# An adaLN trunk with two gated linear attentions: the gate's row as rounded parts, squares added by VectorE, and a free list that ranks tiles behind a store later

## The chip, the cores and the metric

One core of one Trainium2 chip runs the whole layer for one sequence. The metric is the device time of one execution in microseconds (us). Before the change three executions took 1219.83, 1215.38 and 1220.5 us, median 1219.83.

## The reference, cut to what matters

The width is D = 1024, the sequence T = 1024, and there is one layer. All values are fp32.

```python
mod = c_act @ ada_w[l] + ada_b[l]
shift, scale, gate = jnp.split(mod, 3, axis=-1)
h = rms_norm(x, norm_w[l]) * (1.0 + scale[:, None, :]) + shift[:, None, :]
proj = h @ w_in[l]
hq, hf, hi, hz, gq, gk, gv, gz, ga, mg = jnp.split(proj, IN_OFFSETS, axis=-1)
y_h = hgrn2_branch(hq, hf, hi, hz, lb_all[l], hgrn_norm_w[l])   # 8 heads, normed over all 1024
y_g = gla_branch(gq, gk, gv, gz, ga, gla_alpha_w[l], gla_alpha_b[l], gla_norm_w[l])   # 4 heads, normed per head
u_h = y_h @ w_branch[l, 0]
u_g = y_g @ w_branch[l, 1]
mg = jax.nn.sigmoid(mg.reshape(B, T, N_BRANCH, D_MODEL))
merged = mg[:, :, 0] * u_h + mg[:, :, 1] * u_g
x = x + gate[:, None, :] * (merged @ w_out[l])
return rms_norm(x, final_norm_w)
```

## The kernel before

**Products.** A product of fp32 matrices is done as three matmuls of rounded parts (type fp32r): hi x hi, hi x lo and lo x hi. `split` (L186 to L198) makes the parts: ScalarE (ACT) casts to hi (L196), VectorE (DVE) subtracts hi to get lo (L197). Weights get the same at L1285 and L1286 (`prep_duo`), factors of the gate stages at L1260 to L1264 (`build`).

**Order of the work.** A stream of jobs feeds TensorE (PE) with the input projection, one column block after another (`Feat`, its matmuls at L541; `Vblk`, L600 to L602; `Vblk2`, L643 to L645). Between the groups of a job's matmuls `Stream.weave` advances two tracks of generators, whose yielded numbers are a wait in such groups. One track holds the attention heads (`attention`, L657 on, with its score matmuls at L715 and on, copies to `scT` at L790 to L796, then `gla_attention` or `hgrn_attention`). The other, in the background, holds `prepare`, which makes differences of activations (`factors`) and sums of weights (`weight_sums`) and stores them to DRAM, and `gate_side`, which computes the row `gate`. After the stream come four gate stages (`last_stages`, matmuls at L1343): the two halves of `mg` for the two gates, and the two branch projections. Each is a product of 2 x 2 blocks done with seven block products instead of eight, on the stored sums and differences. The first, b = 0, makes the second branch's gate: `put_gate1` takes the sigmoid (L1414) and stores the result (L1415) to DRAM, to be loaded again two stages later. The next, b = 1, makes the other gate (`put_gate0`). Last comes the output projection (`out_stage`, L1520). From the text of the kernel a scheduler derives the order of the instructions of each engine; dependences become semaphores.

**Queues.** Loads are issued by SyncE (SP), in order, so a load that waits holds those behind it. Stores are issued by GpSimd (POOL): `put_act` (L916) for the heads' outputs, `factors` (L1167), `weight_sums` (L1201), `put_gate1` (L1415), `keep_wy` (L1469).

**Slots.** All larger tiles, 46 slots of 4 KB per partition, come from `Slots` (L35 to L53). Freed slots go to the end of a queue, and `get` takes its head: the slot that was freed first. Freeing happens in the text of the kernel, not in time. Whoever writes the next tile in a slot waits for the last readers of the former one, and a store that sends the former tile to DRAM is such a reader. `Halves` (L56 to L80) hands out halves of a slot.

**The gate's row.** In `gate_side` DVE sums eight rows of blocks of `ada_w`, weighted with the conditioning, into `gacc` (L1054, 128 partitions x 1024). Then, for each half of the row, PE sums the partitions and adds the bias with two matmuls in fp32: `ones` x `gacc` (L1062) and one row of `ones` x `gbias` (L1063). ACT copies the result (L1064).

**Squares.** A GLA head has two tiles of squares, added by POOL (L987); the eight HGRN heads add theirs to one tile, by POOL too (L1107, seven adds). Both are followed, at once or at the last head, by `inverse_root`, which splits the sum and sums its partitions on PE. A tile of squares is freed behind its add.

Of the kernel before, what the change touches and what calls it, by code (L numbers as in the profile page):

```python
# [2 lines left out]

# [31 lines left out]
class Slots:  # L35


    def __init__(self, pool, n):
        self.pool = pool
        self.free_list = deque(range(n))  # L40
        self.owner = {}
        self.serial = 0

    def get(self, shape, dtype=F32):
        i = self.free_list.popleft()
        self.serial += 1
        t = self.pool.tile([P] + list(shape), dtype, tag=f"s{i}", name=f"b{self.serial}")
        self.owner[id(t)] = (i, t)
        return t

    def free(self, *tiles):
        for t in tiles:
            self.free_list.append(self.owner.pop(id(t))[0])  # L53


class Halves:  # L56
# [5 lines left out]
    def get(self):  # L62
        if not self.open:
            t = self.slots.get([2, 512])
            left = [0, t]
            self.open.extend((t[:, i, :], left) for i in range(2))
        v, left = self.open.popleft()
        left[0] += 1
        self.owner[id(v)] = (v, left)
        return v  # L70

    def free(self, *views):
        for v in views:
            v, left = self.owner.pop(id(v))
            left[0] -= 1
            if left[0]:
                self.open.append((v, left))
            else:
                self.open = deque(z for z in self.open if z[1] is not left)
                self.slots.free(left[1])  # L80


@with_exitstack
def hybrid_trunk_kernel(
# [6 lines left out]
    nc = tc.nc  # L91
# [822 lines left out]
    def put_act(acts, d, y):  # L914
        for half in range(2):
            nc.gpsimd.dma_start(acts[half][d // 2][:, d % 2 * 512:d % 2 * 512 + 512], y[:, half * 512:half * 512 + 512])  # L916
        S.free(y)

    def alpha_side():
        lower_bound()  # L920
# [49 lines left out]
    def gla_attention(h):  # L970
        qk = g_state
        v = qk.pop(("v", h))
        g = {}
        sq = {}

        def post(vh, half, po):
            if half == 0:
                g[vh] = qk.pop(("z", h, vh))
                sq[vh] = S.get([T])
            sl = slice(half * 512, half * 512 + 512)  # L980
            nc.scalar.activation(sq[vh][:, sl], po, AF.Square)
            nc.vector.scalar_tensor_tensor(g[vh][:, sl], po, vec[:, R_GN + vh:R_GN + vh + 1],
                                           g[vh][:, sl], ALU.mult, ALU.mult)

        yield from attention(qk.pop(("q", h)), qk.pop(("k", h)), alphas[h], lambda: v, 0, 256, post)
        S.free(*v)
        nc.gpsimd.tensor_add(sq[0], sq[0], sq[1])  # L987
        yield 1.5
        rst = sq[1]
        yield from inverse_root(rst, sq[0], 256)  # L990
        for half in range(4):
            sl = slice(half * 256, half * 256 + 256)
            for vh in range(2):
                nc.vector.tensor_mul(g[vh][:, sl], g[vh][:, sl], rst[:, sl])
            yield 1.5
        for vh in range(2):
            put_act(yg_d, 2 * h + vh, g[vh])
        S.free(*sq.values())
# [45 lines left out]
    def gate_side():  # L1044

        gacc, gbias = S.get([D]), S.get([D])
        nc.sync.dma_start(gbias[0:1, :], ada_b[0:1, 2 * D:3 * D])
        for k in range(KT):
            b = S.get([D])
            nc.sync.dma_start(b, ada_w[0, k * P:(k + 1) * P, 2 * D:3 * D])  # L1050
            if k == 0:
                nc.vector.tensor_scalar_mul(gacc, b, cs[:, 0:1])
            else:
                nc.vector.scalar_tensor_tensor(gacc, b, cs[:, k:k + 1], gacc, ALU.mult, ALU.add)  # L1054
            S.free(b)
            yield 1
        yield 3
        gate_b[0] = S.get([D])
        for half in range(2):
            sl = slice(half * 512, half * 512 + 512)  # L1060
            pg = mtile()
            nc.tensor.matmul(pg, ones, gacc[:, sl], start=True, stop=False)  # L1062
            nc.tensor.matmul(pg, ones[0:1, :], gbias[0:1, sl], start=False, stop=True)  # L1063
            nc.scalar.copy(gate_b[0][:, sl], pg)  # L1064
        S.free(gacc, gbias)


    h_state = {}
# [17 lines left out]
    def hgrn_attention(h):  # L1086
        st = h_state
        y = [None]
        sq = [None]

        def post(vh, half, po):
            if half == 0:
                y[0], sq[0] = st.pop(("z", h)), S.get([T])
            sl = slice(half * 512, half * 512 + 512)
            nc.scalar.activation(sq[0][:, sl], po, AF.Square)
            nc.vector.scalar_tensor_tensor(y[0][:, sl], po, vec[:, R_HN + h:R_HN + h + 1],
                                           y[0][:, sl], ALU.mult, ALU.mult)

        yield from attention(st.pop(("q", h)), st.pop(("k", h)), st.pop(("f", h)), lambda: st[("v", h // 4)],
                             h % 4 * P, P, post, 4 if h % 4 == 1 else 3)  # L1100
        if h % 4 == 3:
            S.free(*st.pop(("v", h // 4)))
        put_act(yh_d, h, y[0])
        if ssq[0] is None:
            ssq[0] = sq[0]
        else:
            nc.gpsimd.tensor_add(ssq[0], ssq[0], sq[0])  # L1107
            S.free(sq[0])
        if h == 7:
            yield 2  # L1110
            rst = S.get([T])
            yield from inverse_root(rst, ssq[0], D)
            S.free(ssq[0])
            rst_h[0] = rst
# [40 lines left out]
    def factors(acts, f):  # L1155
        sub = nc.vector.tensor_sub
        for kk in range(2):
# [7 lines left out]
            for p, dst, a, b in ((5, "11", "12", "11"), (7, "12", "12", "22"), (6, "22", "22", "11"), (4, "21", "21", "22")):  # L1165
                sub(y[dst], y[a], y[b])
                nc.gpsimd.dma_start(f[p][kk], y[dst])  # L1167
                if p == 7:
                    S.free(y["12"])
                elif p == 6:  # L1170
                    S.free(y["11"])
                yield 1.5
            S.free(y["22"], y["21"])

    def branch(n, d):
        return w_branch[0, n, :, d * P:(d + 2) * P]
# [6 lines left out]
    def weight_sums(b, i):  # L1183
# [16 lines left out]
        for p, q in SUMS.items():  # L1200
            nc.gpsimd.dma_start(w_sums[b][i // 2][q][:, i % 2 * 512:i % 2 * 512 + 512],  # L1201
                                parts[p].rearrange("p k f -> p (k f)"))
        S.free(x1, x2, s1, s2)
        yield 3

    def prepare():
# [83 lines left out]
    class Banks:  # L1290
# [11 lines left out]
        def free(self, v):  # L1302
            self.free_list.append(v)
# [108 lines left out]
    def put_gate1(d, half, ap, summed):  # L1412
        g = ap if summed else Q.get()
        nc.scalar.activation(g, ap, AF.Sigmoid)  # L1414
        nc.gpsimd.dma_start(gate1_d[d][:, half * 512:half * 512 + 512], g)  # L1415
        Q.free(g)

    def put_gate0(d, half, ap, summed):
        nc.scalar.activation(merged(d, half), ap, AF.Sigmoid)
# [65 lines left out]
        keep_wy(p, kk, *dst)  # L1485

    def drop_wy():
        S.free(*wy.values())
        wy.clear()

    def load_w4(p):
# [191 lines left out]
    stream.hooks[1, 4] = begin_2  # L1683
    stream.go()
    S.free(*h_hi, *h_lo)
    lent = [dtile() for _ in range(2)]
    R.lend([pd[:, i * 512:i * 512 + 512] for pd in lent[::-1] for i in range(2)])
    last_stages()
# [30 lines left out]
```

## Time and profile before

| | before |
|---|---|
| profiled execution, whole | 1216.46 us |
| its span, first to last instruction | 1214.8 us |
| granted TensorE clock | 0.998 |
| PE busy | 1184.1 us, 97% |
| DVE, ACT, POOL busy | 790.9, 546.9, 123.8 us |
| input projection and attention until about | 806 us |
| gate stages and branch projections, then output | 806 to 1214.8 us |

A row of the timeline reads: start, duration (both in us from the start of the span), engine, line, operation, written tile <- read tiles, sizes and type, count, and in brackets how long its engine had been idle and what ended that. Buffer numbers are left out, so most tiles are called `b`; `pd`, `pm` and `sc_ps` are PSUM tiles. PEld is PE's loading of weights, SPq the issuing of loads by SP. A wait for several semaphores is put down to the one that came last.

### The profile page before, as it was taken

The page shows a single profiled execution, that of the slowest core. Times are in us where ns is not written, and L with a number is a line of the kernel's source. Part 1 is how long each engine was busy: PE and PEld are TensorE (multiplying, and loading weights), DVE is VectorE, ACT ScalarE, POOL GpSimd, SP SyncE. Part 2 cuts the span into 40 slices and gives each one's busy share as a digit, 9 for nine tenths or more (in the row PEclk, how much of TensorE's full clock was granted, in tenths as well). Part 3 has the DMA queues.
Part 4 walks back from the last instruction along what each step waited for, and adds up shares of the span by engine and source line. Part 5 has one row for each costly group of instructions (what it writes and reads, how often), then busy time and mean ns, then how long its engine had stood idle before and what let it go on. Part 6 is the DMA issues. An engine that isn't in the chain of part 4 may idle for free.

```text
span 1214.8 us, 20860 instructions
## 1 busy us (share of the span) xinstructions
PE 1184.1 (97%) x8579; PEld 982.6 (81%) x8579; DVE 790.9 (65%) x1245; ACT 546.9 (45%) x797; POOL 123.8 (10%) x215
## 2 busy tenths in 40 slices
PE   5999999999999999999999999999999999999997
PEld 3777889889798888888887888877778888878886
DVE  4637444774848456877884365794653775988994
ACT  5646732434434244344332324455743544444554
POOL 4100000202111121121110101011220000000000
PEclk9999999999999999999999999999999999999999
DMA  9814000844444267255341112054697746435523
GB/s 320 277 70 139 18 19 19 293 141 161 156 152 149 66 207 249 94 179 169 108 174 47 59 53 70 36 174 158 227 343 277 260 160 208 135 104 173 174 104 122
DMA packets 130961, 183.51 MB, mean 151 GB/s; under 512 B 7467, under 2 KB 97633, under 8 KB 130866
## 3 DMA queue, kind: packets, MB, share of 16 engines
q1 hardware_dynamic: 117250, 136.87, 35.7%
q0 software_dynamic: 13568, 45.31, 9.6%
q8 instruction: 67, 1.10, 0.4%
q14 instruction: 28, 0.23, 0.1%
q10 hardware_dynamic: 48, 0.01, 0.0%
HBM read 132.87 MB, written 49.28 MB: 150 GB/s over the span
## 4 chain that ended last, share of the span: by engine, by line
PE 61%; issue 23%; DVE 3%; ACT 3%; POOL 2%; DMA 1%; POOLq 0%; ACTq 0%; DVEq 0%
PE pd L541 19%; PE pd L1343 9%; PE sc_ps L1343 5%; PE pm L1343 5%; PE pd L1520 3%; PE pd L643 2%; PE pd L644 2%; PE pd L645 2%; PE sc_ps L1520 2%; PE pm L848 1%; PE pd L352 1%; PE pm L829 1%; PE pm L850 1%; PE pm L1520 1%; PE sc_ps L352 1%
## 5 line engine op out<-in xcount | busy, mean ns | idle before, releaser
L541 PE MATMUL pd<-b,b 128*128 128x512 f32 x1632 | 387.4, 394 | 0.0
L541 PEld LDWEIGHTS pd<-b,b 128*128 128x128 f32 x1632 | 302.4, 188 | 64.8 <-issue 1.4
L1343 PE MATMUL pd<-b,b 128*128 128x512 f32 x720 | 173.7, 392 | 4.3 <-ACT b L1414 2.1
L1343 PEld LDWEIGHTS pd<-b,b 128*128 128x128 f32 x720 | 133.7, 188 | 35.7 <-ACT b L1414 3.2
L197 DVE TENSOR_TENSOR b<-b,b 128x1024 fp32r<-128x1024 f32 (+2 forms) x89 | 98.9, 1122 | 83.1 <-ACT b L196 65.4
L196 ACT CAST b<-b 128x1024 fp32r<-128x1024 f32 (+2 forms) x89 | 82.9, 948 | 92.1 <-DVE b L1199 14.6
L1286 DVE TENSOR_TENSOR b<-b,b 128x1024 fp32r<-128x1024 f32 x56 | 68.3, 1224 | 66.9 <-ACT b L1285 52.3
L1285 ACT CAST b<-b 128x1024 fp32r<-128x1024 f32 x56 | 58.3, 1050 | 73.9 <-PE pd L1343 20.6
L1343 PE MATMUL sc_ps<-b,b 128*128 128x512 f32 x324 | 79.4, 391 | 1.0 <-ACT scT L793 1.0
L600 PE MATMUL pd<-b,b 128*128 128x256 f32 x256 | 74.2, 290 | 0.0
L1264 DVE TENSOR_TENSOR b<-b,b 128x1024 fp32r<-128x1024 f32 x48 | 59.2, 1251 | 20.8 <-ACT b L1263 15.1
L602 PE MATMUL pd<-b,b 128*128 128x256 f32 x256 | 72.5, 283 | 0.0
L601 PE MATMUL pd<-b,b 128*128 128x256 f32 x256 | 72.4, 283 | 0.0
L1343 PEld LDWEIGHTS sc_ps<-b,b 128*128 128x128 f32 x324 | 60.3, 188 | 14.6 <-ACT scT L793 1.4
L1343 PE MATMUL pm<-b,b 128*128 128x512 f32 x300 | 72.1, 389 | 0.0
L1263 ACT CAST b<-b 128x1024 fp32r<-128x1024 f32 x48 | 49.9, 1050 | 41.2 <-PE pd L1343 16.0
L1343 PEld LDWEIGHTS pm<-b,b 128*128 128x128 f32 x300 | 56.3, 188 | 11.7
L352 PE MATMUL pd<-b,b 128*128 128x512 f32 x192 | 53.3, 410 | 2.0 <-ACT b L196 0.9
L1201 POOL DMA_DIRECT2D ws<-b x64 | 34.6, 541 | 192.0 <-DVE b L1195 86.5
L735 ACT COPY xb<-b 128x512 f32<-128x512 f32 x48 | 29.4, 620 | 49.4 <-PE sc_ps L715 26.7
L643 PE MATMUL pd<-b,b 128*128 128x512 f32 x128 | 51.3, 401 | 0.0
L644 PE MATMUL pd<-b,b 128*128 128x512 f32 x128 | 50.0, 390 | 0.0
(285 smaller groups left out, 1964.3 us busy)
## 6 DMA issues: line engine op xcount, KB each, us to landing
b<-in_w_in_dram SPq DMA_DIRECT2D x66, 512.0 KB, 4.2
ws<-b POOLq DMA_DIRECT2D x64, 256.0 KB, 3.3
b<-ws SPq DMA_DIRECT2D x32, 512.0 KB, 4.9
b<-in_x_dram SPq DMA_DIRECT2D x16, 512.0 KB, 5.7
b<-in_ada_w_dram SPq DMA_DIRECT2D x32, 256.0 KB, 6.9
b<-in_w_branch_dram SPq DMA_DIRECT2D x16, 512.0 KB, 4.4
b<-h SPq DMA_DIRECT2D x14, 512.0 KB, 4.3
wo<-b POOLq DMA_DIRECT2D x14, 512.0 KB, 5.7
```

The source lines that it names most:

```text
L196: nc.scalar.copy(hi, src)
L197: nc.vector.tensor_sub(lo, src, hi.bitcast(F32))
L352: nc.tensor.matmul(accs[f], wg(a, d, f), b[d][:, half * 512:half * 512 + 512], start=(d == 0 and n == 0), stop=(d == KT - 1 and n == 2))
L541: nc.tensor.matmul(ps[0:w, th * 512:(th + 1) * 512], a[:, k, 0:w], b[:, th * 512:(th + 1) * 512], start=(k == 0 and n == 0), stop=(k == KT ...
L600: nc.tensor.matmul(o, lh, hi[:, k % 4, :], start=(k == 0), stop=False)
L601: nc.tensor.matmul(o, lh, lo[:, k % 4, :], start=False, stop=False)
L602: nc.tensor.matmul(o, ll, hi[:, k % 4, :], start=False, stop=(k == KT - 1))
L643: nc.tensor.matmul(o, lh, hi[:, k % 2, :], start=(k == 0), stop=False)
L644: nc.tensor.matmul(o, lh, lo[:, k % 2, :], start=False, stop=False)
L1286: nc.vector.tensor_sub(lo, t, hi.bitcast(F32))
L1343: nc.tensor.matmul(o, a[:, sl], c, start=(p in (1, 5) and kt == 0 and n == 0), stop=(kt == 3 and n == 2), skip_group_check=True)
L1520: nc.tensor.matmul(o, a, b, start=(p in (1, 5) and kt == 0 and n == 0), stop=(kt == 3 and n == 2), skip_group_check=True)
```

## The change

It has three parts.

1. *Gate's row.* DVE adds the bias to the first partition's row of `gacc`, `split` makes hi and lo of the sum (ACT and DVE), and four fp32r matmuls, `ones_r` x hi and `ones_r` x lo for each half, take the place of four fp32 ones. Two more slots are taken for it, and the generator yields 4 instead of 3 ahead of the matmuls.
2. *Squares.* The eleven adds go from POOL to DVE.
3. *Free list.* It becomes a heap, ranked by the count of tiles handed out at the time of freeing. Tiles that a store still reads are marked `sent` and get `S.behind` added to their rank. `S.behind` is 0 until the stream has ended, where the order is that of the queue before, and 8 from the gate stages on.

```diff
--- before.py
+++ after.py
@@ -1,3 +1,4 @@
+import heapq
 from collections import deque
 from contextlib import ExitStack
 
@@ -37,20 +38,22 @@
 
     def __init__(self, pool, n):
         self.pool = pool
-        self.free_list = deque(range(n))
+        self.free_list = [(-1, i - n, i) for i in range(n)]
+        self.freed = self.behind = 0
         self.owner = {}
         self.serial = 0
 
     def get(self, shape, dtype=F32):
-        i = self.free_list.popleft()
+        i = heapq.heappop(self.free_list)[-1]
         self.serial += 1
         t = self.pool.tile([P] + list(shape), dtype, tag=f"s{i}", name=f"b{self.serial}")
         self.owner[id(t)] = (i, t)
         return t
 
-    def free(self, *tiles):
+    def free(self, *tiles, sent=False):
         for t in tiles:
-            self.free_list.append(self.owner.pop(id(t))[0])
+            self.freed += 1
+            heapq.heappush(self.free_list, (self.serial + (self.behind if sent else 0), self.freed, self.owner.pop(id(t))[0]))
 
 
 class Halves:
@@ -62,22 +65,23 @@
     def get(self):
         if not self.open:
             t = self.slots.get([2, 512])
-            left = [0, t]
+            left = [0, t, False]
             self.open.extend((t[:, i, :], left) for i in range(2))
         v, left = self.open.popleft()
         left[0] += 1
         self.owner[id(v)] = (v, left)
         return v
 
-    def free(self, *views):
+    def free(self, *views, sent=False):
         for v in views:
             v, left = self.owner.pop(id(v))
             left[0] -= 1
+            left[2] |= sent
             if left[0]:
                 self.open.append((v, left))
             else:
                 self.open = deque(z for z in self.open if z[1] is not left)
-                self.slots.free(left[1])
+                self.slots.free(left[1], sent=left[2])
 
 
 @with_exitstack
@@ -914,7 +918,7 @@
     def put_act(acts, d, y):
         for half in range(2):
             nc.gpsimd.dma_start(acts[half][d // 2][:, d % 2 * 512:d % 2 * 512 + 512], y[:, half * 512:half * 512 + 512])
-        S.free(y)
+        S.free(y, sent=True)
 
     def alpha_side():
         lower_bound()
@@ -984,7 +988,7 @@
 
         yield from attention(qk.pop(("q", h)), qk.pop(("k", h)), alphas[h], lambda: v, 0, 256, post)
         S.free(*v)
-        nc.gpsimd.tensor_add(sq[0], sq[0], sq[1])
+        nc.vector.tensor_add(sq[0], sq[0], sq[1])
         yield 1.5
         rst = sq[1]
         yield from inverse_root(rst, sq[0], 256)
@@ -1054,15 +1058,18 @@
                 nc.vector.scalar_tensor_tensor(gacc, b, cs[:, k:k + 1], gacc, ALU.mult, ALU.add)
             S.free(b)
             yield 1
-        yield 3
+        nc.vector.tensor_add(gacc[0:1, :], gacc[0:1, :], gbias[0:1, :])
+        hi, lo = split(gacc)
+        S.free(gacc, gbias)
+        yield 4
         gate_b[0] = S.get([D])
         for half in range(2):
             sl = slice(half * 512, half * 512 + 512)
             pg = mtile()
-            nc.tensor.matmul(pg, ones, gacc[:, sl], start=True, stop=False)
-            nc.tensor.matmul(pg, ones[0:1, :], gbias[0:1, sl], start=False, stop=True)
+            nc.tensor.matmul(pg, ones_r, hi[:, sl], start=True, stop=False)
+            nc.tensor.matmul(pg, ones_r, lo[:, sl], start=False, stop=True)
             nc.scalar.copy(gate_b[0][:, sl], pg)
-        S.free(gacc, gbias)
+        S.free(hi, lo)
 
 
     h_state = {}
@@ -1104,7 +1111,7 @@
         if ssq[0] is None:
             ssq[0] = sq[0]
         else:
-            nc.gpsimd.tensor_add(ssq[0], ssq[0], sq[0])
+            nc.vector.tensor_add(ssq[0], ssq[0], sq[0])
             S.free(sq[0])
         if h == 7:
             yield 2
@@ -1166,11 +1173,11 @@
                 sub(y[dst], y[a], y[b])
                 nc.gpsimd.dma_start(f[p][kk], y[dst])
                 if p == 7:
-                    S.free(y["12"])
+                    S.free(y["12"], sent=True)
                 elif p == 6:
-                    S.free(y["11"])
+                    S.free(y["11"], sent=True)
                 yield 1.5
-            S.free(y["22"], y["21"])
+            S.free(y["22"], y["21"], sent=True)
 
     def branch(n, d):
         return w_branch[0, n, :, d * P:(d + 2) * P]
@@ -1200,7 +1207,8 @@
         for p, q in SUMS.items():
             nc.gpsimd.dma_start(w_sums[b][i // 2][q][:, i % 2 * 512:i % 2 * 512 + 512],
                                 parts[p].rearrange("p k f -> p (k f)"))
-        S.free(x1, x2, s1, s2)
+        S.free(x1, x2)
+        S.free(s1, s2, sent=True)
         yield 3
 
     def prepare():
@@ -1413,7 +1421,7 @@
         g = ap if summed else Q.get()
         nc.scalar.activation(g, ap, AF.Sigmoid)
         nc.gpsimd.dma_start(gate1_d[d][:, half * 512:half * 512 + 512], g)
-        Q.free(g)
+        Q.free(g, sent=True)
 
     def put_gate0(d, half, ap, summed):
         nc.scalar.activation(merged(d, half), ap, AF.Sigmoid)
@@ -1485,7 +1493,7 @@
         keep_wy(p, kk, *dst)
 
     def drop_wy():
-        S.free(*wy.values())
+        S.free(*wy.values(), sent=True)
         wy.clear()
 
     def load_w4(p):
@@ -1683,6 +1691,7 @@
     stream.hooks[1, 4] = begin_2
     stream.go()
     S.free(*h_hi, *h_lo)
+    S.behind = 8
     lent = [dtile() for _ in range(2)]
     R.lend([pd[:, i * 512:i * 512 + 512] for pd in lent[::-1] for i in range(2)])
     last_stages()
```

Three places of the resulting order. On PE, at the matmuls of the gate's row (`pm` the sum, `pd` the tile of the job in the stream), before:

```order
L644 MATMUL pd_5955<-b_5712,b_150 128x512
L645 MATMUL pd_5955<-b_5711,b_158 128x512
L1062 MATMUL pm_6017<-b_5918,ones 128x512
L1063 MATMUL pm_6017<-b_5919,ones 128x512
L1062 MATMUL pm_6021<-b_5918,ones 128x512
L1063 MATMUL pm_6021<-b_5919,ones 128x512
L643 MATMUL pd_6026<-b_5699,b_143 128x512
L644 MATMUL pd_6026<-b_5700,b_143 128x512
```

and now, where lines of the file are a few higher:

```order
L648 MATMUL pd_6022<-b_5700,b_143 128x512
L649 MATMUL pd_6022<-b_5699,b_151 128x512
L647 MATMUL pd_6022<-b_5699,b_144 128x512
L648 MATMUL pd_6022<-b_5700,b_144 128x512
L649 MATMUL pd_6022<-b_5699,b_152 128x512
L1069 MATMUL pm_6030<-b_5999,ones_r 128x512
L1070 MATMUL pm_6030<-b_6000,ones_r 128x512
L1069 MATMUL pm_6034<-b_5999,ones_r 128x512
L1070 MATMUL pm_6034<-b_6000,ones_r 128x512
L647 MATMUL pd_6022<-b_5703,b_145 128x512
```

The four have moved behind six matmuls of the next `pd` tile, and read the two parts.

On ACT, at the start of the gate stages (L1260 and L1268 the rounding of a factor's part 3, L1285 and L1293 the cast of weights, L1414 and L1422 the sigmoid, L1317 and L1325 a copy of a finished bank, L735 and L739 copies for a head), before:

```order
L1317 ACTIVATE b_7505<-pd_7440 128x512
L1317 ACTIVATE b_7601<-pd_7441 128x512
L735 COPY xb<-b_7164 128x512
L735 COPY xb<-b_7330 128x512
L735 COPY xb<-b_7164 128x512
L735 COPY xb<-b_7330 128x512
L1317 ACTIVATE b_7601<-pd_7441 128x512
L1414 ACTIVATE b_7638<-pd_7440 128x512
L1260 ACTIVATE b_7823<-b_7755 128x1024
L1414 ACTIVATE b_7731<-pd_7440 128x512
L1285 CAST b_7913<-b_7807 128x1024
L790 COPY scT<-sc_ps 32x4x32 x4
```

and now:

```order
L1268 ACTIVATE b_7828<-b_7760 128x1024
L1325 ACTIVATE b_7606<-pd_7446 128x512
L739 COPY xb<-b_7169 128x512
L739 COPY xb<-b_7335 128x512
L739 COPY xb<-b_7169 128x512
L739 COPY xb<-b_7335 128x512
L1325 ACTIVATE b_7606<-pd_7446 128x512
L1422 ACTIVATE b_7643<-pd_7445 128x512
L1293 CAST b_7871<-b_7743 128x1024
L1422 ACTIVATE b_7736<-pd_7445 128x512
L1293 CAST b_7918<-b_7812 128x1024
L794 COPY scT<-sc_ps 32x4x32 x4
```

The second rounding, of `b_7823` and now `b_7828`, stands ahead of the copies to `xb` instead of behind the first sigmoid, and where it stood is a cast of weights.

On SP, late in the first gate stage (`fx` stored factors, `ws` stored sums, `in_w_in_dram` weights), before:

```order
L1230 DMA b_8082<-fx_736 128x1024
L1278 DMA b_8061<-in_w_in_dram 128x4x128 x2
L1230 DMA b_8081<-fx_735 128x1024
L1278 DMA b_8110<-in_w_in_dram 128x4x128 x2
L1278 DMA b_8159<-in_w_in_dram 128x4x128 x2
L1278 DMA b_8200<-in_w_in_dram 128x4x128 x2
L1466 DMA b_8328<-in_w_out_dram 128x2x512
L1274 DMA b_8347<-ws_749 128x1024
L1278 DMA b_8237<-in_w_in_dram 128x4x128 x2
```

and now:

```order
L1238 DMA b_8086<-fx_735 128x1024
L1238 DMA b_8087<-fx_736 128x1024
L1286 DMA b_8066<-in_w_in_dram 128x4x128 x2
L1286 DMA b_8115<-in_w_in_dram 128x4x128 x2
L1286 DMA b_8205<-in_w_in_dram 128x4x128
L1286 DMA b_8164<-in_w_in_dram 128x4x128 x2
L1286 DMA b_8205<-in_w_in_dram 128x4x128
L1286 DMA b_8242<-in_w_in_dram 128x4x128 x2
L1282 DMA b_8312<-ws_745 128x1024
```

The two loads of `b_8159`, now `b_8164`, stood third and fourth of six; now one of the two loads of the next tile, `b_8205`, stands ahead of them. Its slot is one that a gate store reads.

## Prediction

> **What bounds the kernel now.** I read the page's totals first, then its slices, then the list of PE's waits, then the timeline at each place where the change or a wait stands.
>
> ```profile
> span 1214.8 us, 20860 instructions
> ...
> PE 1184.1 (97%) x8579; PEld 982.6 (81%) x8579; DVE 790.9 (65%) x1245; ACT 546.9 (45%) x797; POOL 123.8 (10%) x215
> ...
> PE   5999999999999999999999999999999999999997
> ...
> PEclk9999999999999999999999999999999999999999
> ```
>
> TensorE (PE) is busy for 97% of the span, full in every slice but the first and the last, and its clock is full throughout. So a change gains where it takes a matmul away, or where it ends one of PE's few waits. What it does on VectorE (DVE, 65%), ScalarE (ACT, 45%) and GpSimd (POOL, 10%) counts only if PE stands still for it. The list of PE's waits (engine, tile and line <- releaser: total, times, longest) says where it does:
>
> ```profile
> PE pd L1343 <- ACT b L1414: 2.1, 2, 1.8
> PE pd L1343 <- DVE b L953: 1.5, 1, 1.5
> ...
> PE sc_ps L1343 <- ACT scT L793: 1.0, 1, 1.0
> ...
> PE pd L1343 <- DVE b L1435: 0.4, 1, 0.4
> ...
> PE sc_ps L715 <- DVE blk L698: 0.2, 1, 0.2
> PE pd L1343 <- ACT b L1315: 0.2, 1, 0.2
> ```
>
> These six are all waits that can belong to the gate stages or to attention heads near an edit; together 5.4 us. The other rows of the list lie at lines that the change doesn't touch. More than 5.4 us can therefore come only from matmuls that cost less.
>
> **The gate's row** is the one place where PE itself gets less work. The timeline of before (start, duration, engine, line, tiles):
>
> ```profile
> 640.47 0.39 PE L644 MATMUL pd<-b,b 128*128 128x512 f32 x1
> ...
> 640.69 0.39 PE L645 MATMUL pd<-b,b 128*128 128x512 f32 x1
> ...
> 640.92 1.02 PE L1062 MATMUL pm<-b,ones 128*128 128x512 f32 x2
> 641.12 1.01 ACT L648 COPY b<-pd 128x1024 f32<-128x1024 f32 x1 [9.86 <-PE pd L645]
> ...
> 641.87 1.12 PE L1063 MATMUL pm<-b,ones 1*128 1x512 f32 x2
> ...
> 644.08 1.04 ACT L196 CAST b<-b 128x1024 fp32r<-128x1024 f32 x1 [0.47 <-PE pm L1062]
> ...
> 645.02 0.50 PE L643 MATMUL pd<-b,b 128*128 128x512 f32 x1
> 645.19 1.23 DVE L197 TENSOR_TENSOR b<-b,b 128x1024 fp32r<-128x1024 f32 x1 [6.22 <-ACT b L196]
> ```
>
> From 640.92 to 645.02 PE does four fp32 products, each in two passes: 4.10 us. The fp32r matmuls ahead of them follow each other at 640.47, 640.69 and 640.92, so every 0.225 us. Four of that kind take 0.90 us: **-3.2 us**. They now need hi and lo of the summed row. The chain: the last of the five accumulations ends at 632.41 + 6.56 = 638.97,
>
> ```profile
> 632.41 6.56 DVE L1054 SCALAR_TENSOR_TENSOR b<-b,cs,b 128x1024 f32<-128x1024 f32 x5
> ```
>
> then the add of the bias (I take the 1.23 us of a 128x1024 DVE operation, though it is one row), the cast (1.04) and the subtraction (1.23): 642.5. The order of instructions puts the four matmuls six later, that is at 640.92 + 6 x 0.225 = 642.3, and the first of them needs hi alone. So the chain is just in time. ACT is idle for 9.86 us before 641.12, so the cast finds it free. Were the copy of 641.12 in front, lo would come at about 644.4 and PE would lose 1.9 of the 3.2 again. Bounds -3.2 to -1.3; I take **-3.1**.
>
> **The eleven adds that go from POOL to DVE.** Such an add is 2.4 us on POOL, and beside each a DVE instruction is long. Two of them, with the group that shows the usual length of one of these DVE lines:
>
> ```profile
> 284.78 2.40 POOL L987 TENSOR_TENSOR b<-b,b 128x1024 f32<-128x1024 f32 x1 [1.16 <-ACT b L981]
> 285.40 2.33 DVE L1198 TENSOR_TENSOR b<-b,b 128x512 f32<-128x512 f32 x1
> 798.04 2.75 POOL L1107 TENSOR_TENSOR b<-b,b 128x1024 f32<-128x1024 f32 x1
> 799.10 2.21 DVE L679 TENSOR_TENSOR xb<-xb,b 128x256 f32<-128x256 f32 x1
> L1198 DVE TENSOR_TENSOR b<-b,b 128x512 f32<-128x512 f32 x16 | 12.6, 788 | 0.1
> ```
>
> Of 16 at L1198 the one beside POOL takes 2.33, so the other 15 take (12.6 - 2.33) / 15 = 0.68: the neighbour loses 1.6 us. On DVE the add itself should take 1.2 us, as the other 128x1024 operations do. Net per add between -0.4 and, if the neighbour's length had another cause, +1.2; I take -0.3, by the rows. The Trainium skill, SBUF — State Buffer, "Who interferes with whom", says that a VectorE instruction with two SBUF inputs and a GpSimd instruction that reads SBUF exclude each other for a whole instruction. By it the neighbour's loss is POOL's doing and goes with the add (the trace agrees: 285.40 + 2.33 ends 0.55 us after POOL's 287.18, about the instruction's own 0.68); without it DVE would carry 11 x 1.2 = 13 us more.
>
> Elsewhere than at 812 us PE has DVE's result in hand, so a few tenths either way cost nothing there; the 0.2 at L698 stays as it is. At 812 DVE has been behind since 799:
>
> ```profile
> 810.62 1.23 DVE L953 TENSOR_TENSOR b<-b,pd 128x1024 f32<-128x1024 f32 x1
> 811.90 1.43 PE L1343 MATMUL pd<-b,b 128*128 128x512 f32 x5 [1.49 <-DVE b L953]
> ```
>
> L953 frees a PSUM bank for which PE waits 1.49. The stretch at 799.10 (2.21, of a kind that is 256 columns wide and so at most the 0.68 of L1198) goes, an add of 1.2 comes: L953 ends 0.3 earlier. But ACT now has a cast ahead of the copy that frees the neighbouring bank. **-0.2**, bounds -1.5 (the wait goes) to +1.2.
>
> **The free list.** Slots that a store still reads are handed out later, so waits for a store move from ACT to other places. Three of ACT's waits stand just before waits of PE. First:
>
> ```profile
> 828.34 1.06 ACT L1260 ACTIVATE b<-b 128x1024 fp32r<-128x1024 f32 x1 [3.59 <-DMA gate<-b]
> 829.43 1.23 DVE L1261 SCALAR_TENSOR_TENSOR b<-b,b 128x1024 fp32r<-128x1024 f32 x1 [0.58 <-ACT b L1260]
> 832.15 1.06 ACT L790 COPY scT<-sc_ps 32x128 f32<-32x128 f32 x4 [1.34 <-DVE blk L785]
> 834.02 1.89 PE L1343 MATMUL sc_ps<-b,b 128*128 128x512 f32 x7 [0.96 <-ACT scT L793]
> 836.19 1.19 PE L1343 MATMUL pd<-b,b 128*128 128x512 f32 x4 [0.28 <-ACT b L1414]
> ```
>
> The rounding at L1260 waits 3.59 us for a gate store, DVE follows it, and with it the blocks that go to scT, and PE. In the new order this rounding stands seven instructions earlier, ahead of the four copies to xb; another cast takes the wait for the store, but DVE no longer hangs on it and needs one operation of 1.23 fewer at that point. scT then comes 1.2 earlier, and both waits of PE go: **-1.2** (bounds -1.24 to 0, if the cast that now waits holds ACT as long).
>
> Second and third:
>
> ```profile
> 857.29 2.00 ACT L1285 CAST b<-b 128x1024 fp32r<-128x1024 f32 x2 [3.07 <-DMA b<-ws]
> 859.83 2.56 PE L1343 MATMUL pd<-b,b 128*128 128x512 f32 x10 [0.15 <-ACT b L1315]
> 889.35 1.05 ACT L1285 CAST b<-b 128x1024 fp32r<-128x1024 f32 x1 [2.33 <-DMA b<-in_w_in_dram]
> 892.22 0.60 ACT L1414 ACTIVATE b<-pd 128x512 f32<-128x512 f32 x1 [0.76 <-DMA gate<-b]
> 892.87 1.43 PE L1343 MATMUL pd<-b,b 128*128 128x512 f32 x5 [1.82 <-ACT b L1414]
> 878.35 6.14 SPq L1278 DMA_DIRECT2D b<-in_w_in_dram x6
> 879.41 0.54 POOL L1415 DMA_DIRECT2D gate<-b  x1 [0.93 <-ACT b L1414]
> gate<-b POOLq DMA_DIRECT2D x16, 256.0 KB, 4.6
> ```
>
> At 859.83 PE's 0.15 goes with ACT's wait: **-0.15**. At 892.87 PE waits 1.82 for a sigmoid, which itself waited 0.76 for a gate store's slot; in the new order it doesn't. But ahead of it on ACT stands the cast of weights that in before starts with their landing (889.35). Their loads, third and fourth of the six that SP issues from 878.35 on, now stand behind the first half of another load, and that half waits for a gate store issued at 879.41, landed some 4.6 later, at 884.0. They would go out up to 2.8 us later than at 881.2, where they go now if the six are issued evenly from 878.35 to 884.49. With a queue that is shorter then, they may land as before. Bounds -1.8 (the wait goes) to +2.1 (2.8 late, less the 0.7 saved); I take **-0.5**, near the row of the wait that goes.
>
> **Sum:** -3.1 - 0.2 - 1.2 - 0.15 - 0.5 = -5.2 us. The profiled execution took 1216.46 us, so 1211.3; it lies 3.4 below the median of the runs, 1219.83, from which the same sum gives 1214.6. As the comparison is with the median I predict **1214.0**. A difference of 0.5% (6.1 us) is about what a measurement can tell from no change here, so this is close to that bound on the near side.
>
> **The rivals.** (a) *Slower: loads held on SP.* SP issues in order; each load that waits for a store's landing holds all behind it. The new order has such waits at four loads between 840 and 900 us. If each lets the next weights land 3 us after PE needs them (the 2.8 above), PE loses 4 x 3 = 12 us against the 5.2 gained: +7, **1227**. It decides from a lateness beyond the time that weights lie ready before their cast. For it: the cast at 889.35 has none. Against it: that is the only such place, and PE's list has no wait for a load in the gate stages. 12%, of which 10 points lie over 0.5%.
> (b) *Only the gate's row pays*: -3 us, **1216.7**; the waits of ACT come back at the casts that now stand before the sigmoids. For it: the cast that takes over the wait at 828. 25%.
> (c) *Everything pays:* all 5.4 us of the listed waits but L1435 and L698 go, so -3.2 - 4.8 = -8.0, **1211.8**. Against it: a wait that ends lets the next one appear. 23%.
> (d) *The DVE adds cost their full 1.2 us* and hold L953: -5.2 + 0.2 + 1.2 = -3.8, **1216.0**, 5%.
> My forecast has 35%.
>
> **Numbers.** Range: from case (c) with the profiled execution's level (1216.46 - 8 = 1208.5), less 1, to no change with the upper run (1220.5): 1207.5 to 1220.5; rival (a) and a little on the lower side stay out. Faster by over 0.5%: case (c), a third of my forecast (its part beyond -6.1), 0.35. Slower: 0.10. Within: 0.55.
>
> **What would show it.** Right: the four matmuls of the gate's row take 0.9 us with no wait before them; no DVE instruction above 2.2 us at the old places; no PE wait at scT L797 or behind L1325; ACT's waits for a gate store gone before the sigmoids, SP's waits longer. Wrong: PE rows that name a load or a cast of weights between 840 and 915 us (rival a), or a wait of about 1.5 us at the same sigmoids (b), or L957 as late as before (d).

## The result and the profile after

The changed kernel takes 1210.12 us (median of 6 runs, 1208.55 to 1210.64), before 1217.54 (6 runs beside it): ratio 0.9943, 95% interval 0.9929 to 0.9957, so 7 us less. A second comparison, beside other kernels, gave 0.9954 (0.9939 to 0.9968), 5.6 us. Forecast were 5.2 us less and 1214.0, in a range of 1207.5 to 1220.5: the time lies in it, and the gain within what the two intervals leave. Not every term came as forecast. Two single executions, one of the kernel before (1479.17 us, clock 0.755) and one of a part of the change (6709.93 us), lie far outside all others and enter no ratio.

The profiled execution took 1208.55 us. Its page, and PE's waits in the stages that the change touches:

```profile
span 1206.8 us, 20832 instructions
...
PE 1179.6 (98%) x8575; PEld 982.2 (81%) x8575; DVE 793.2 (66%) x1258; ACT 548.4 (45%) x798; POOL 95.2 (8%) x204
```

```profile
PE sc_ps L1351 <- ACT scT L797: 1.5, 1, 1.5
...
PE pd L1351 <- DVE b L957: 1.0, 1, 1.0
...
PE pd L1351 <- ACT b L1422: 0.8, 2, 0.5
```

PE is busy 4.5 us less. Of the waits named in the prediction, the sigmoid's went from 2.1 to 0.8, L957's (before L953) from 1.5 to 1.0, the copy of a bank (L1315) is gone, and so are the 0.2 at L698, which was to stay, and `sc_ps <- tot`, 0.7, which the prediction had left out. The wait for scT, forecast to go, is longer: 1.5 instead of 1.0.

To see where the time came from I took the same matmul in both profiles and subtracted its start in the changed kernel from its start in before. This difference, the lead of the changed kernel, grows in steps:

| at (time in before) | lead, us | step | place |
|---|---|---|---|
| 20 | 1.0 | | the start, same instructions; 0 in the second profile of the changed kernel |
| 107 | 1.3 | 0.2 | |
| 312 to 331 | 2.2 | 0.9 | attention's wait for `tot` |
| 551 | 2.5 | 0.3 | attention, L698's wait |
| 646 | 5.8 | 3.3 | gate's row (2.9 in the second profile) |
| 813 | 6.1 | 0.4 | L957 |
| 832 | 5.6 | -0.5 | scT |
| 857 | 6.1 | 0.5 | bank copies |
| 894 | 7.35 | 1.25 | the sigmoid (0.6 in the second profile) |
| 1206 | 7.5 | 0.2 | |

The gate's row, in order of time:

```profile
637.33 1.05 ACT L200 CAST b<-b 128x1024 fp32r<-128x1024 f32 x1 [6.49 <-DVE b L1061]
...
638.41 1.22 DVE L201 TENSOR_TENSOR b<-b,b 128x1024 fp32r<-128x1024 f32 x1 [1.12 <-ACT b L200]
...
639.59 0.39 PE L649 MATMUL pd<-b,b 128*128 128x512 f32 x1
...
639.82 0.39 PE L1069 MATMUL pm<-b,ones_r 128*128 128x512 f32 x1
...
640.75 0.39 PE L647 MATMUL pd<-b,b 128*128 128x512 f32 x1
```

Four matmuls from 639.82 to 640.75: 0.93 us where there were 4.10, and no wait. lo is ready at 639.63, and the second matmul, the first that reads it, starts at 640.05.

The attention at 312: before, PE waits for `tot`, which DVE makes. After, DVE adds the squares, waits for a store of `yg`, and PE has no wait:

```profile
313.46 0.89 PE L715 MATMUL sc_ps<-xb,b 128*32 128x48 f32 x64 [0.66 <-DVE tot L718]
```

```profile
284.10 1.22 DVE L991 TENSOR_TENSOR b<-b,b 128x1024 f32<-128x1024 f32 x1
...
286.37 0.68 DVE L1205 TENSOR_TENSOR b<-b,b 128x512 f32<-128x512 f32 x1
...
303.81 0.69 DVE L1203 TENSOR_TENSOR b<-b,b 128x512 f32<-128x512 f32 x1 [3.50 <-DMA yg<-b]
...
311.44 0.89 PE L719 MATMUL sc_ps<-xb,b 128*32 128x48 f32 x64
```

The add takes 1.22 on DVE, its neighbour (L1205, before L1198 with 2.33) now 0.68, and PE's wait is gone.

scT, and the sigmoid near 892:

```profile
817.87 0.32 SPq L1238 DMA_DIRECT2D b<-fx  x1
...
818.90 0.54 POOL L1423 DMA_DIRECT2D gate<-b  x1 [24.66 <-ACT b L1422]
...
824.19 1.05 ACT L1293 CAST b<-b 128x1024 fp32r<-128x1024 f32 x1 [5.58 <-DMA gate<-b]
825.14 0.59 ACT L1422 ACTIVATE b<-pd 128x512 f32<-128x512 f32 x1
825.63 1.04 ACT L1293 CAST b<-b 128x1024 fp32r<-128x1024 f32 x1
826.56 1.06 ACT L794 COPY scT<-sc_ps 32x128 f32<-32x128 f32 x4
...
828.43 1.88 PE L1351 MATMUL sc_ps<-b,b 128*128 128x512 f32 x7 [1.50 <-ACT scT L797]
```

```profile
883.41 1.05 ACT L1293 CAST b<-b 128x1024 fp32r<-128x1024 f32 x1 [2.10 <-DMA b<-in_w_in_dram]
884.37 0.62 ACT L1422 ACTIVATE b<-b 128x512 f32<-128x512 f32 x1
884.89 0.58 ACT L1422 ACTIVATE b<-pd 128x512 f32<-128x512 f32 x1
885.52 3.01 PE L1351 MATMUL pd<-b,b 128*128 128x512 f32 x12 [0.52 <-ACT b L1422]
```

A cast now waits for the store instead of the rounding, for longer, and holds ACT, so scT comes when the store has landed plus three instructions. At 884 the sigmoid waits for no store any more, only for ACT, which had waited 2.10 us for the weights.

### The profile page after: what moved, and what is told of

It is laid out like the page before. It is cut to its first block, busy times and chain, and to the rows that moved or that the text cites. A ratio compares the mean times of both kernels' runs of the same rounds, so it can differ in the third digit from the quotient of the medians.

```text
span 1206.8 us, 20832 instructions
## 1 busy us (share of the span) xinstructions
PE 1179.6 (98%) x8575; PEld 982.2 (81%) x8575; DVE 793.2 (66%) x1258; ACT 548.4 (45%) x798; POOL 95.2 (8%) x204
## 4 chain that ended last, share of the span: by engine, by line
PE 47%; issue 39%; POOL 3%; DMA 2%; DVE 2%; ACT 2%; SPq 0%; POOLq 0%; ACTq 0%; DVEq 0%
PE pd L1351 9%; PE pd L545 9%; PE sc_ps L1351 5%; PE pm L1351 5%; PE pd L1528 3%; PE pd L606 2%; PE pd L605 2%; PE pd L604 2%; POOL ws L1208 2%; PE sc_ps L1528 2%; DMA b<-in_w_in_dram 2%; PE pd L356 1%; PE pm L1528 1%; PE pm L852 1%; PE pm L854 1%
## 5 line engine op out<-in xcount | busy, mean ns | idle before, releaser
L1293 ACT CAST b<-b 128x1024 fp32r<-128x1024 f32 x56 | 58.7, 1051 | 64.6 <-PE pm L1351 20.0
L739 ACT COPY xb<-b 128x512 f32<-128x512 f32 x48 | 29.4, 620 | 48.9 <-PE sc_ps L719 26.8
```

The costliest lines, as they stand in the source:

```text
L1293: nc.scalar.copy(hi, t)
```

## The experiments

Theory A: each part pays by itself, by the steps above. Its rivals are named with each run. The times of the experiments are beside runs of before on the same chip (medians 1216.1 to 1216.5). The eight combinations of the three parts, in two numbers from each profile, the start of the first matmul of the gate stages and the time from there to the start of the last one (b = 0 to 3), and the ratio. The first two are from one profile each, and a profiled execution lies up to 2.7 us off the median of its kernel (row and adds: 1214.92 against 1212.26), so differences of 1 or 2 us between them say little.

| kernel | gate stages begin | they last | ratio (95%) |
|---|---|---|---|
| before | 806.06 | 324.07 | 1 |
| gate's row alone | 802.27 | 323.99 | 0.9976 (0.9966 to 0.9986) |
| adds alone | 805.14 | 325.41 | 1.0005 (0.9997 to 1.0014) |
| list alone | 807.31 | 325.16 | 1.0001 (0.9992 to 1.0010) |
| row and adds | 802.39 | 326.13 | 0.9968 (0.9958 to 0.9979) |
| row and list | 803.36 | 327.17 | 0.9986 (0.9976 to 0.9996) |
| adds and list | 804.83 | 324.71 | 0.9987 (0.9977 to 0.9996) |
| all, two profiles | 800.28, 802.21 | 322.27, 322.88 | 0.9943, 0.9954 |

**Gate's row alone.**

```diff
+        nc.vector.tensor_add(gacc[0:1, :], gacc[0:1, :], gbias[0:1, :])
+        hi, lo = split(gacc)
...
-            nc.tensor.matmul(pg, ones, gacc[:, sl], start=True, stop=False)
-            nc.tensor.matmul(pg, ones[0:1, :], gbias[0:1, sl], start=False, stop=True)
+            nc.tensor.matmul(pg, ones_r, hi[:, sl], start=True, stop=False)
+            nc.tensor.matmul(pg, ones_r, lo[:, sl], start=False, stop=True)
```

> Only the gate's row is changed. Theory A (each part pays by itself, as the two profiles' steps put it): 3.2 us less than before (ratio 0.997), all of it at the four matmuls, which take 0.9 us together. Rival B (the parts pay only together, because without the DVE adds moved the chain add, cast, subtraction comes late): a wait of 1 to 2 us before these matmuls, and only 1 to 2 us less.

2.9 us less. PE does wait for lo, though less than rival B says. One reason is POOL's add, beside which DVE's accumulation is long:

```profile
623.09 2.43 POOL L1110 TENSOR_TENSOR b<-b,b 128x1024 f32<-128x1024 f32 x1
```

```profile
623.16 3.44 DVE L1054 SCALAR_TENSOR_TENSOR b<-b,cs,b 128x1024 f32<-128x1024 f32 x1
```

```profile
641.81 0.50 PE L1066 MATMUL pm<-b,ones_r 128*128 128x512 f32 x1 [0.44 <-DVE b L197]
```

The accumulation ends 1.1 us after POOL's add, about its own length (1.27). It isn't the only reason: with the row and the adds, where no add is left on POOL, PE waits too, since DVE has waited for a load of `ada_w` (DVE, then PE):

```profile
630.71 1.29 DVE L1058 SCALAR_TENSOR_TENSOR b<-b,cs,b 128x1024 f32<-128x1024 f32 x1 [0.97 <-DMA b<-in_ada_w_dram]
...
641.93 0.50 PE L1070 MATMUL pm<-b,ones_r 128*128 128x512 f32 x1 [0.33 <-DVE b L201]
```

In the other seven profiles with the row and the adds DVE waits 0 to 0.65 us for that load, and the matmul that reads lo starts 0 to 0.2 us late. Theory A holds for the time; the chain is just in time, and POOL's add or the load can make it up to 0.6 us late.

**Adds alone.**

```diff
-        nc.gpsimd.tensor_add(sq[0], sq[0], sq[1])
+        nc.vector.tensor_add(sq[0], sq[0], sq[1])
...
-            nc.gpsimd.tensor_add(ssq[0], ssq[0], sq[0])
+            nc.vector.tensor_add(ssq[0], ssq[0], sq[0])
```

> Only the eleven adds go to DVE. Theory A: the neighbours on DVE lose their 1.0 to 1.6 us each, the adds take 1.2 us each, and the time is 0.3 to 1.3 us less than before (the steps of 0.75, 0.27 and 0.36 us at 311, 551 and 812 us in the changed kernel, if all belong to the adds). Rival C (the adds cost DVE their full length): 1 us or more slower, with L957's counterpart later than before.

No difference, and neither theory as it stood. Up to the gate stages it gains 0.9 us, 0.7 of it at 311. The 0.3 at 551 isn't the adds' doing: the row alone and the list alone gain 0.2 there with the adds still on POOL. The gate stages take 1.3 longer, by several small waits, of which these two were shorter in before (1.5 and 1.0):

```profile
PE pd L1343 <- DVE b L953: 1.6, 1, 1.6
PE sc_ps L1343 <- ACT scT L793: 1.3, 1, 1.3
```

**List alone.** Only `Slots`, `Halves`, `sent=True` and `S.behind = 8` of the diff.

> Only the free list is changed. Theory A: about 1.2 us less than before (plus 0.5 at 832, minus 0.5 at 857, minus 1.25 at 894, as in the changed kernel). Rival D (the list gains only where the adds have already made DVE early): no change, within 0.5 us, and the wait for the sigmoid near 892 stays at 1.5 us or more. Rival E (the store's landing is what decides at 828): PE still waits over 1 us for scT.

No difference; rival D is right about the time, though not about the sigmoid's wait (1.3, not 1.5 or more). One thing that it loses shows in the profile (ACT, then PE):

```profile
852.98 1.04 ACT L200 CAST b<-b 128x1024 fp32r<-128x1024 f32 x1 [1.53 <-POOL b L1111]
853.93 0.58 ACT L1320 COPY b<-pd 128x512 f32<-128x512 f32 x1
```

```profile
854.56 3.02 PE L1348 MATMUL pd<-b,b 128*128 128x512 f32 x12 [1.46 <-ACT b L1320]
```

The new order puts the cast of the summed squares ahead of a bank's copy. With the sum still on POOL the cast waits 1.53 for it, and PE 1.46 for the bank. PE waited 0.6 for scT, not over 1, so rival E's number failed.

**Row and adds; row and list; adds and list.** The first has 0 in place of 8, the second leaves the adds on POOL, the third leaves the row.

> The gate's row and the adds, with the number 0 in place of 8, so that the free list is the queue of before. The gate's row alone gave 2.9 us, the adds alone lost 0.6, the list alone lost 0.1. If the parts add up: 2.3 us less than before. If adds and gate's row pay together (DVE freed ahead of 640 us): 4 us or more less.

> The gate's row and the list with its 8; the adds stay on POOL. If the parts add up: 2.8 us less than before. Theory G (the list pays only where the adds have left POOL, as with the list alone a cast waited for POOL's add and held a bank's copy, 1.5 us of PE at 854): about 3 us less, with that wait of PE at 1 us or more near 850, against 6 for the whole change. Rival H (the list pays with the gate's row, since its two more slots shift which slot goes to which tile): 5 us or more less, without that wait.

> The adds and the list with its 8; the gate's row as before. The last of the eight combinations. If the list pays wherever the adds have left POOL: 1.7 us (as with the gate's row, 3.9 against 5.6) less than the adds alone, so 1 us less than before, with PE's wait for the sigmoid near 892 under 1 us. If it pays only with the two more slots of the gate's row: no change or slower, with that wait at 1.5 us or more.

3.9, 1.7 and 1.6 us less. With row and adds, the sigmoid waits for the store's slot as before:

```profile
888.86 0.60 ACT L1422 ACTIVATE b<-pd 128x512 f32<-128x512 f32 x1 [1.35 <-DMA gate<-b]
```

```profile
889.51 4.22 PE L1351 MATMUL pd<-b,b 128*128 128x512 f32 x12 [1.94 <-ACT b L1422]
```

With row and list, POOL's adds cost twice, at the bank's copy as above (1.46) and at L957 (DVE, POOL, PE):

```profile
795.16 3.10 DVE L689 TENSOR_TENSOR b<-b,b 128x256 f32<-128x256 f32 x1
```

```profile
795.35 2.40 POOL L1114 TENSOR_TENSOR b<-b,b 128x1024 f32<-128x1024 f32 x1
```

```profile
810.09 1.25 PE L1351 MATMUL pd<-b,b 128*128 128x512 f32 x4 [2.39 <-DVE b L957]
```

Of the whole change L957 keeps PE 1.0 us; here a neighbour loses 2.5 (3.10 against 0.63 without POOL) where the add would cost 1.2, and the wait is 1.4 longer. POOL isn't all of it: the row alone, with its adds on POOL too, has 1.45 at this place. Theory G is right about the wait at the bank, though 1.7 us less is not its 3. With adds and list PE still waits 1.2 for the sigmoid.

The gate's row matters to these stages too, though its work lies ahead of them: at L957 PE waits 0.9 to 1.05 us in all eight profiles with the row and the adds, and 1.4 to 2.4 in the six others. Whether this comes by its two more slots was not tried apart.

Some waits cost more than their length. In row and list the 24 matmuls from 810.09 take 7.55 us, in before 5.73: from 811.09 on they follow each other every 0.425 us, not every 0.23, while the granted clock of PE is half (one stretch of 1 us: PE busy and its matmuls, granted clock, share and rate of DMA):

```profile
812.00:813.00 1.00, 1.00 (x4) 0.50 0.75 184
```

The clock is half for 3.4 us there, as long with row and adds (from 891.1), with adds and list (812.1) and with 16 (902.5), and for 6.8 us with 12 (888.1), each time at or just behind a wait of PE of 1.6 to 3.8 us. In the nine other profiles it is full in the gate stages. With adds and list 20 matmuls then take 6.37 us, with the adds alone 4.83, so about 1.5 us are lost beyond the wait. It doesn't always come: with 4 PE waits 2.40 us, and the 24 matmuls behind take 5.78.

So the parts don't add up: row, adds and list alone make 2.2 us, together 5.6 to 7. For the stream, the profiles have 3.8, 0.9 and -1.3 us alone and 3.9 to 5.8 together, but their leads differ by 1.3 us already at 20 us, so they can't tell. The gate stages differ by the waits of each order of slots, and in five of the profiles by the clock.

**The number: 4, 12, 16.**

```diff
-    S.behind = 8
+    S.behind = 16
```

> The changed kernel with 4 in place of 8. With 0 it gave 3.9 us less than before, with 8 it gave 5.6, with 16 nothing. Theory J (the number trades waits of ACT for a store, below 8, against loads held on SP, above it, and 8 lies between): 4 to 6 us less than before, with a wait for the sigmoid near 892 that is still over 1 us, and no wait of PE for a cast of weights. Rival K (each number is a new draw of slots, with no trend): anything from 2 us to 7 us less, with waits at places that fit neither side.

> The changed kernel with 12 in place of 8. Theory J: between 8 (5.6 us less than before) and 16 (0): 2 to 4 us less, with SP held for several us behind a load whose slot a store still reads, and PE waiting for a cast of weights near 900 us. Rival K: as fast as with 8 or faster, or a wait at another place.

> The changed kernel with the number 16 in place of 8: a slot behind a store is handed out 16 tiles later. The cast that waited 5.58 us for a gate store ahead of scT now stands behind the copies to scT. Theory A (ACT's wait for that store is all that holds scT): PE's wait of 1.5 us at scT goes to under 0.3, and the kernel is 1.0 to 1.5 us faster than the changed one, if nothing new waits: 1208.7. Rival F (the wait only moves: loads on SP are held, or slots come round too soon for other readers): as fast as the changed kernel or up to 2 us slower, with a new wait of PE between 840 and 1000 us.

Ratios 0.9976 (0.9966 to 0.9986), 0.9990 (0.9981 to 1.0000) and 0.9999 (0.9989 to 1.0009). With 4, ACT waits 7.16 us for a gate store at a cast ahead of copies of banks, and PE 2.4 for them; for the sigmoid near 892 PE doesn't wait at all, so the place is not the one expected:

```profile
909.28 1.99 ACT L1293 CAST b<-b 128x1024 fp32r<-128x1024 f32 x2 [7.16 <-DMA gate<-b]
```

With 12, the wait stands at the very sigmoid and cast of the prediction's rival (a): the cast ahead of it waits for weights whose load SP issued late. Of PE's 5.34 us behind the wait, 2.3 are the halved clock's (3.02 in before).

```profile
888.32 1.04 ACT L1293 CAST b<-b 128x1024 fp32r<-128x1024 f32 x1 [2.52 <-DMA b<-in_w_in_dram]
889.27 0.59 ACT L1422 ACTIVATE b<-pd 128x512 f32<-128x512 f32 x1
```

```profile
889.91 5.34 PE L1351 MATMUL pd<-b,b 128*128 128x512 f32 x12 [3.77 <-ACT b L1422]
```

With 16 the cast ahead of scT is gone, as theory A says (PE waits 0.3 for scT, and gains 1.2 there), but SP stands for most of 8.9 us between two loads of `ws`, and all is lost again at 901 (SP, ACT, PE):

```profile
883.55 8.94 SPq L1282 DMA_DIRECT2D b<-ws  x2
```

```profile
899.38 1.99 ACT L1293 CAST b<-b 128x1024 fp32r<-128x1024 f32 x2 [7.19 <-DMA b<-in_w_in_dram]
```

```profile
901.42 0.73 PE L1351 MATMUL pd<-b,b 128*128 128x512 f32 x2 [2.16 <-ACT b L1293]
```

The kinds of wait are those of theory J: ACT waits for a store below 8, SP holds loads above. Its sizes are not (2.9 us less with 4, forecast were 4 to 6; 1.2 with 12, forecast were 2 to 4). Places and sizes jump (rival K): the gate stages last 326.1, 325.7, 322.6, 327.0 and 327.2 us for 0, 4, 8, 12 and 16 (with the halved clock in 0, 12 and 16), and the ratios of 0 and 4 are alike within their intervals, so 8 is not the middle of a slope.

**Sixteen for the first two blocks only**, then 8.

```diff
-    S.behind = 8
+    S.behind = 16
...
+    after(0, 2, 1, lambda: setattr(S, "behind", 8))
```

> The changed kernel with 16 until the second of the four column blocks of the second product of the first gate stage, and 8 from there on. Only two things change in the instructions' order: the cast that waited 5.58 us for a gate store ahead of scT stands behind the copies to scT, and one load of a factor stands ahead of two others. Theory A: PE's wait at scT goes from 1.5 to about 0.3, the late waits of the kernel with 16 throughout don't come, and the time is about 1.1 us under the changed kernel's. Rival F (the slot's wait comes back at another cast or load): no faster than the changed kernel, with a new wait of PE between 832 and 860 us.

Ratio 0.9943 (0.9930 to 0.9956), 1209.22 us; beside the same runs of before the changed kernel has 0.9954 and 1210.91. The gate stages last 321.1 us, the shortest of all. Only the wait for scT changed:

```profile
829.70 1.89 PE L1351 MATMUL sc_ps<-b,b 128*128 128x512 f32 x7 [0.29 <-ACT scT L797]
```

Lead over the changed kernel's profile at this place: 1.2 us, and no step elsewhere in the gate stages. So what held scT was the cast that waited for the store. By its median this is the best full version that I ran, though the two intervals overlap.

**One add left out**, that of head 6, whose squares are then missing from the norm.

```diff
-            nc.vector.tensor_add(ssq[0], ssq[0], sq[0])
+            if h != 6:
+                nc.vector.tensor_add(ssq[0], ssq[0], sq[0])
```

> The changed kernel without the sixth of the seven adds of the HGRN heads' squares (the one at 793 us; its head's squares are left out of the norm's sum). DVE is gapless from there to the add at L957, for which PE waits 1.0 us at 806. Theory A (an add costs DVE 1.2 us, and here all of it is on the path): that wait goes, and the kernel is 1.0 us faster than the changed one. Rival I (something else ends late there, such as ACT's cast ahead of it): the wait stays at 0.7 or more, and the time with it.

```profile
807.16 1.22 DVE L957 TENSOR_TENSOR b<-b,pd 128x1024 f32<-128x1024 f32 x1 [0.26 <-ACT b L956]
```

```profile
808.44 3.83 PE L1352 MATMUL pd<-b,b 128*128 128x512 f32 x15 [0.87 <-DVE b L957]
```

The wait stays, 0.87, and DVE now idles for ACT: rival I. A DVE instruction less is worth 0.2 us here, as ACT's chain of casts ends almost as late. (Ratio 0.9943, 0.9927 to 0.9959; it overlaps the changed kernel's, so the time says nothing.)

## Why the prediction was right, and where not

*Gate's row, -3.1:* 3.2 us are saved by the matmuls, and 2.9 by this part alone. Right, with its bound: the chain is just in time, and in five of the ten profiles with this part it is 0.1 to 0.6 us late.

*Adds, -0.3 each on DVE, nothing elsewhere, -0.2 at 812:* the lengths were right. DVE has 13 instructions more (eleven adds, the bias, the subtraction), of 1.2 us each, 15.9, and is busy 2.3 us more: 13.6 went, with the stretched neighbours. At 812 the gain was 0.4, but only together with the row; with the adds alone L953 kept PE 1.6 us. "Elsewhere than at 812 us" nothing was to change, and this was wrong: the adds gained up to 0.7 us at 311. The step that failed stands at the first view: "The other rows of the list lie at lines that the change doesn't touch." The row `sc_ps <- tot L718`, 0.7 us, was one of them; its line isn't touched, but DVE's work ahead of it is. The four profiles with the adds on POOL have this wait, with 0.32 to 0.66 us; none of the ten with the adds on DVE has it. The Trainium skill, SBUF — State Buffer, "Who interferes with whom", has it that the loser of the shared port waits until the other's instruction ends: the accumulation at 623.16 above, which ends 1.1 us after POOL's add, agrees.

The traces show how the adds reach `tot`. Before and after (SP, then DVE):

```profile
293.66 2.19 SPq L1189 DMA_DIRECT2D b<-in_w_in_dram  x2
...
301.72 0.69 DVE L1195 TENSOR_TENSOR b<-b 128x512 f32<-128x512 f32 x1 [0.71 <-DMA b<-in_w_in_dram]
...
305.98 0.69 DVE L1196 TENSOR_TENSOR b<-b,b 128x512 f32<-128x512 f32 x1 [3.56 <-DMA yg<-b]
```

```profile
292.37 1.38 SPq L1196 DMA_DIRECT2D b<-in_w_in_dram  x2
...
299.63 0.68 DVE L1202 TENSOR_TENSOR b<-b 128x512 f32<-128x512 f32 x1
```

The stretched neighbours on DVE make the last sum of weights, and its store to `ws`, 0.5 us later by the kernel's own clock. SP's second load goes out at 295.85, just when that store has landed, and in the changed kernel 0.8 us earlier. DVE waits 0.5 to 0.7 us for this load in the four profiles with the adds on POOL, at most 0.12 in the ten others, and its next wait ends 4.7 to 5.0 us after the store of `yg` is issued in the four, 4.0 to 4.3 in the ten. That the later load is what holds up the store of `yg` fits, but no run took it apart.

*Scores' copies, -1.2:* became +0.5. The step that failed: "another cast takes the wait for the store, but DVE no longer hangs on it". DVE was indeed early, but ACT, which copies scT, stood behind that cast. This was the bound named there ("if the cast that now waits holds ACT as long"), and it went beyond, since the store freed ACT 5.3 us after its issue (818.90 to 824.19), in before 3.3 (825.04, the store's issue, to 828.34). What differs is a load of `fx` issued at 817.87. In the seven profiles where ACT waits for this store and such a load goes out 1.0 to 1.8 us ahead, it is 4.2 to 5.4; in the five without the load, 2.9 to 3.6. No run moved the load alone.

*The copy at 859, -0.15:* -0.45 in both profiles, so mis-sized. The list counts a wait from the end of the matmul ahead, which it puts 0.39 us behind its start, though the next could start 0.23 behind it. In before the starts at 859.28, 859.83 and 860.16 are 0.55 and 0.33 apart, so that the wait of 0.15 cost 0.42. *The sigmoid at 892, -0.5:* -1.25 and -0.6 in the two profiles. The mechanism was right; what is left of its wait is the weights' landing, as the bound on the slow side said.

*Rivals.* (a) is real: with 12 PE waited 3.8 us at the place foretold, where it had waited 1.8 in before, and with 16 it undid the change. With 8 the loads came almost in time (PE lost 0.5 at 885 us). (b) and (c) were each partly right, since one wait came back and an unlisted one went; (d) was wrong for the whole change, where L957's wait is shorter. What the prediction didn't weigh is that the parts need each other: it took the sum of parts, and two parts alone give nothing. That the total came out is in part luck. The five terms of the sum measured 4.9 us in the first profile and 3.8 in the second, not 5.2; the rest came from the attention (1.2 and 1.0), which was put at nothing, and, in the first profile, from 1.0 at the start, which is chance.

The level: the sum gave 1214.6 from the median, and the 0.6 from there to the 1214.0 forecast stands on no row. Before ran from 1213.9 to 1220.5 us, over more than 80 runs, the changed kernel from 1208.55 to 1211.7. Some of it goes with the clock: of the runs of before, the seven with a mean granted clock of 0.996 took 1216.8 to 1220.5, the nine with 0.999 took 1214.9 to 1217.6; the changed kernel's twelve have 0.998 or 0.999. So a part of the gain may be that the halved clock comes less often, which the one profile of before doesn't show. Some is chance in when a store lands, as in the kernel without one add, at instructions equal to the others' (DVE, then PE):

```profile
377.41 1.23 DVE L201 TENSOR_TENSOR b<-b,b 128x1024 fp32r<-128x1024 f32 x1 [2.83 <-DMA ws<-b]
```

```profile
382.96 0.89 PE L719 MATMUL sc_ps<-xb,b 128*32 128x48 f32 x64 [1.60 <-DVE tot L722]
```

In the changed kernel's first profile the same instruction waited 1.07 and PE not at all.

## What to carry to other kernels

Follow a shared wait to the engine that takes it over, and ask who else stands behind it there: moving a wait from a rounding to a cast is no gain while the same engine makes both. A rule that hands out buffers is a schedule: test it in the full combination and at several values, and look for the one wait that it leaves (here 16 for two blocks) before turning its number for all. When a wait has cost more than its length, look at the clock of the stretch behind it. And read the list of PE's waits for what stands ahead of each, not for the line that it names.

## What the runs showed of the hardware

An operation on one partition, the bias's add (1x1024), took 1.21 us, no less than 1.22 for 128 partitions. A store of 256 KB freed its waiting engine 2.9 to 3.6 us after its issue, and 4.2 to 5.4 with a load of 512 KB issued 1.0 to 1.8 us ahead of it. The granted clock of PE fell to half for 3.4 or 6.8 us at or behind five waits of 1.6 to 3.8 us, and not behind another of 2.4.
